# Eight experts in one order of load: which of them are split, and which one comes first

## The chip, the core and the metric

The program runs on one core of one Trainium2 chip. The metric is device time in microseconds (us) of one execution, from the first to the last instruction with what lies around it. Four compute engines work side by side, each in its own fixed order: TensorE (PE, with its weight loads as PEld), VectorE (DVE), ScalarE (ACT) and GpSimd (POOL). SyncE (SP) issues nearly all transfers, also in a fixed order. An instruction that has to wait holds up everything behind it on its own engine.

## The reference

256 tokens of width 1024 pass two blocks of two layers. The change touches the last stage alone, a layer with eight experts, of which each token takes the two with the largest logits:

```python
def swiglu(x, w_gu, w_down):
    g, u = jnp.split(x @ w_gu, 2, axis=-1)
    return (jax.nn.silu(g) * u) @ w_down

def moe_ffn(x, router, w_gu, w_down):
    ...
    logits = (xt @ router).astype(jnp.float32)
    top_v, top_i = lax.top_k(logits, TOP_K)
    w = jax.nn.softmax(top_v, axis=-1)
    ...
    for e in range(N_EXPERTS):
        y = y + combine[:, e:e + 1] * swiglu(xt, w_gu[e], w_down[e])
```

An expert is 3 x 1024 x 3584 weights in fp32, that is 42 blocks of 1 MiB; all eight are 336 MiB (352.3 MB). For the inputs of this case the reference sends 63, 135, 103, 26, 69, 94, 6 and 16 tokens to experts 0 to 7, or, by size, 135, 103, 94, 69, 63 (expert 0), 26, 16 and 6.

## The kernel before

Everything ahead of the expert layer (two hybrid layers, a pooling layer, a dense layer, an attention layer) is the same in both kernels and takes the first 1100 us. Then `moe_layer` (L1555 and on) does this.

**Routing.** `Route.choose` ranks the logits of 128 tokens at a time; `place` gives each token its slot in its expert's list; `route_order` (L1174 to L1221) sorts the experts by load, makes the table `R` of slots and weights in the sorted order, and casts the sorted expert numbers into `ri` (L1212). SP reads a number from `ri` into a register (`value_load` in `begin`, L1363) and uses it as the address of that expert's weights. A constant `first` adds 1000 to the count of expert 0, so that expert 0 always takes place 0 of the order, whatever its load. Its address is therefore known without routing (`E.static`), and its loads stand in SP's queue ahead of any read of `ri`.

**Two ways to compute an expert.** A place in the order has a fixed number of slots.
- A *split* place (slots 128, or 128 and another 64 for the place of 192): the slots' rows of x are gathered by a product with a selection matrix (`gather_x`); each 1 MiB of weights is cut by ACT into a high part `whi` (L148) and by DVE into a low part `wlo` (L149), and PE multiplies in three passes (`mm3`, L210 to L212). The further 64 slots take two passes (`prod`, L1324 and L1325).
- An *unsplit* place (64 or 32 slots): fp32 weights go to PE as they were loaded, with two (64) or four (32) products side by side in the columns of the array (`prod_full`, L1333), and `fold` adds the partial sums on ACT and DVE.

Before, the places are: 0 (expert 0) split 128; 1 split 192; 2, 3, 4 split 128; 5 unsplit 64; 6, 7 unsplit 32. With the loads above the split places hold 63, 135, 103, 94, 69 and the unsplit ones 26, 16, 6. If any load exceeds its place, a branch at the end (`over`, L1647) computes the rest; here it isn't taken.

**Buffers and order.** Loads go round seven buffers of 1 MiB (`raw`); besides, `K.spare` sends one load in eight (more at the start) into places that are otherwise unused (the table at L1574). Split parts have four buffers each. Two generators run through the experts in steps of 512 hidden columns, each of three parts (gate, up, down; 21 parts for an expert): one over places 0 to 4, one over 6, 7, 5. The second is advanced by a rate per part of the first (`rate`, L1635: 0.4 during place 0, 1.4 during place 1, 0.48 then), which mixes unsplit parts among the split ones. A scheduler then fixes the order of each engine.

Of the kernel before, what the change touches and what calls it, by code (L numbers as in the profile page):

```python
# [9 lines left out]
F32 = mybir.dt.float32  # L10
# [8 lines left out]
KT = D // 128  # L19
# [32 lines left out]
def _consts():  # L52
# [36 lines left out]
    for g in range(2):  # L89
        for q in range(64):  # L90
# [9 lines left out]
                ("first", np.tile([1000.0] + [0.0] * 7, (128, 1))),  # L100
                ("lim", np.array([[128.0, 192, 128, 256, 256, 64, 32, 256]])),
# [1070 lines left out]
def route_order(K, pool, S):  # L1172
# [21 lines left out]
    cnt = sc(8)  # L1194
    nc.vector.tensor_tensor(cnt, Q[:, 1, :], cst("first"), op=OP.add)
# [69 lines left out]
def gather_x(K, pool, x, R, p, tl, n, between=None):  # L1265

    half = tl.kind == "h"
    dbl = 2 if n == 0 else 1
    nc = K.nc
    m = tl.m  # L1270
    xg = buffer(K, pool, f"xg{n}", 0, *([[128, KT, m], F32] if tl.full else [[128, KT, m // 64, 128], F32R]), dbl)
    if between is None:
        if tl.P is None:
            select(K, pool, R, p, tl)
        steps = [(k, t) for k in range(KT) for t in range(2)]
    else:
        select(K, pool, R, p, tl, [0])
        K.hold_at[K.loads + 2] = [K.last]
        steps = [(k, t) for t in range(2) for k in range(KT)]
    ps = {}  # L1280
    hold = []
    for k, t in steps:
        if between is not None and (k, t) == (4, 0):
            hold = [between()]
            select(K, pool, R, p, tl, [1])
        if t == 0 and k % 4 == 0:
            ps[k] = bank(K, "mm")[:, :4 * m].rearrange("p (a b) -> p a b", a=4)
        k0 = k - k % 4
        with behind(K, hold):
            nc.tensor.matmul(ps[k0][:, k % 4, :], x[:, t, k * 128:(k + 1) * 128], tl.P[:, t, :m],  # L1290
                             start=t == 0 and (between is None or k % 4 == 0),
                             stop=t == 1 and (between is None or k % 4 == 3))
        if t == 0 or k % 4 < 3:
            continue
        if tl.full:
            nc.scalar.activation(xg[:, k0:k0 + 4, :], ps[k0], AF.Copy)
        elif half:
            evac_hl(K, xg[:, k0:k0 + 4, 0, 0:64], xg[:, k0:k0 + 4, 0, 64:128], ps[k0])
        else:
            evac_hl(K, xg[:, k0:k0 + 4, 0, :], xg[:, k0:k0 + 4, 1, :], ps[k0])  # L1300
    tl.xg = xg
# [45 lines left out]
class Expert:  # L1347
    def __init__(self, p, tiles):
        self.p, self.tiles = p, [Tile(*t) for t in tiles]
        self.static = 0 if p == 0 else None  # L1350
        self.full = self.tiles[0].full


def run_experts(K, pool, A, x, R, ri, cw, y, experts, hook=None, last=False):
# [5 lines left out]
    def begin(E):  # L1360
        if E.static is None:
            with behind(K, K.line):
                e = nc.sync.value_load(ri[0:1, E.p:E.p + 1], min_val=0, max_val=NE - 1)  # L1363
        else:
# [194 lines left out]
def moe_layer(K, x, A, out, ps1, S):  # L1559
    nc = K.nc  # L1560
    with ExitStack() as es:
# [6 lines left out]
        with K.tc.tile_pool(name="exp", reuse_waits="tile", bufs=1) as ep:  # L1568
# [16 lines left out]
            gather_w(K, ep, cw, 0, E[0].tiles[0], 0)  # L1585
# [8 lines left out]
            E[1].tiles[1].sb = True  # L1594
            ahead = [(1, 0), (1, 1)]
            slots = {6: 0, 7: 32, 5: 64}

            def few():

                b = ep.tile([128, 2048], F32, name="box2", tag="box2")  # L1600
                xg = b[:, 0:1024].rearrange("p (k m) -> p k m", m=128)
                K.boxes["sgl"] = [b[:, c:c + 512] for c in (1024, 1536)]
                P = b[:, 1536:1792].rearrange("p (t m) -> p t m", t=2)
                for p, c in slots.items():
                    tl = E[p].tiles[0]
                    select(K, ep, R, p, tl)
                    for t in range(2):
                        nc.vector.tensor_copy(P[:, t, c:c + tl.m], tl.P[:, t, :tl.m])
                    gather_w(K, ep, cw, p, tl, f"l{p}")
                    tl.xg = xg[:, :, c:c + tl.m]  # L1610
                for k0 in range(0, KT, 4):
                    ps = bank(K, "mm").rearrange("p (a b) -> p a b", a=4)
                    for k in range(k0, k0 + 4):
                        for t in range(2):
                            nc.tensor.matmul(ps[:, k % 4, :], x[:, t, k * 128:(k + 1) * 128], P[:, t, :],
                                             start=t == 0, stop=t == 1)
                    nc.scalar.activation(xg[:, k0:k0 + 4, :], ps, AF.Copy)

            def boxes():
                b = [ep.tile([128, 2048], t, name=f"box{n}", tag=f"box{n}") for n, t in enumerate((F32R, F32))]  # L1620
                K.boxes["xg1"] = [b[0][:, 0:1024].rearrange("p (k o m) -> p k o m", o=1, m=128)]
                K.boxes["hT1"] = [b[0][:, c:c + 512].rearrange("p (k o m) -> p k o m", o=1, m=128) for c in (1024, 1536)]
                K.boxes["sg1"], K.boxes["sacc"] = [b[1][:, c:c + 512] for c in (0, 512)], [b[1][:, 1024:2048]]

            def hook(i):
                if i == 3:
                    few()
                if i == 4:
                    boxes()
                if 3 <= i < len(ahead) + 3:  # L1630
                    p, n = ahead[i - 3]
                    select(K, ep, R, p, E[p].tiles[n])
                if 4 <= i < len(ahead) + 4:
                    p, n = ahead[i - 4]
                    gather(K, ep, x, R, cw, p, E[p].tiles[n], n)  # L1635

            light, done, due = go([E[6], E[7], E[5]]), 0, 0.0
            rate = (0.4, 1.4, 0.48, 0.48, 0.48)
            for e, f in go([E[q] for q in (0, 1, 2, 3, 4)], hook, True):
                if E[5].tiles[0].xg is not None:  # L1640
                    due += rate[e.p]
# [5 lines left out]
            with K.tc.If(over > 0):  # L1647
                K.line = []
                rest = ((0, F1), (1, H(192)), (2, F1), (3, H(128)), (5, H(64)), (6, H(32)), (7, H(32)))
# [126 lines left out]
```

## Time and profile before

| what | value |
|---|---|
| runs | 2082.11, 2083.7, 2084.06 us; median 2083.7 us |
| profiled execution | 2082.68 us; its span 2080.7 us, so 1.98 us lie around the span |
| PE busy | 1998.4 us (96% of the span) |
| DVE, ACT busy | 1349.0 us (65%), 1029.1 us (49%) |
| moved from HBM | 520.73 MB, mean 251 GB/s over the span |
| expert layer | PE from about 1115 us on, the last loads issued at 2034.9 us |

The page's row of PE's busy share counts matmuls whose ends are modelled, so a share near 100% in a stretch doesn't say that PE did all it can there; the starts of its instructions, and how far apart they are, say more. The page's two rows of the DMA (busy share and GB/s in 40 slices) show two halves: some 170 GB/s up to 1100 us, and 320 to 420 GB/s after, where the expert weights are loaded.

### The profile page before, as it was taken

Reading aid. Unit: us, or ns where it says so; the run is one execution under the profiler, and the core shown is the slowest. Engines: PE = TensorE matmul, PEld = TensorE weight load, DVE = VectorE, ACT = ScalarE, POOL = GpSimd, SP = SyncE. Lnnn points to the kernel's source line nnn. Section 1 sums busy time; section 2 is a strip of 40 time slices with the busy share of each in tenths; the row PEclk is TensorE's granted clock in tenths of the full one; section 3 lists DMA queues with packets and bytes.
Section 4 is the critical chain, followed back from the end, with each engine's and each line's share of the span. In section 5 each row is a group of like instructions: output and inputs, shape, how many; then the busy total and the mean of one; then the engine's idle time right before and its main releaser. Section 6 shows DMA issues by size and latency. Waiting matters only on the chain. (4 is left out here: it accounts for less than half of the span.)

```text
span 2080.7 us, 28322 instructions
## 1 busy us (share of the span) xinstructions
PE 1998.4 (96%) x11287; PEld 1586.8 (76%) x11287; DVE 1349.0 (65%) x1722; ACT 1029.1 (49%) x1222; POOL 34.8 (2%) x39
## 2 busy tenths in 40 slices
PE   8999999999999899999899999999999999999996
PEld 7879998888999899988778876567666766665664
DVE  6866545876545644566659775656577777656756
ACT  6654444664444433345335665445355555545543
POOL 0000000000001100000000000000000000000000
PEclk9999999999999999999878999999999999999998
DMA  9434554535555455550406799999899999999993
GB/s 342 156 102 150 176 182 177 182 108 187 175 200 182 163 182 183 170 193 21 167 1 243 323 374 385 370 349 401 337 401 371 392 423 380 355 346 364 373 379 104
DMA packets 137851, 523.69 MB, mean 252 GB/s; under 512 B 12016, under 2 KB 44144, under 8 KB 94832
## 3 DMA queue, kind: packets, MB, share of 16 engines
q1 hardware_dynamic: 137568, 521.75, 66.5%
q8 instruction: 90, 1.47, 0.3%
q14 instruction: 49, 0.40, 0.1%
q10 hardware_dynamic: 144, 0.07, 0.0%
HBM read 520.73 MB, written 1.05 MB: 251 GB/s over the span
## 5 line engine op out<-in xcount | busy, mean ns | idle before, releaser
L149 DVE TENSOR_TENSOR wlo<-raw,whi 128x2048 fp32r<-128x2048 f32 (+2 forms) x346 | 739.8, 2159 | 295.4 <-ACT whi L148 295.0
L148 ACT ACTIVATE whi<-raw 128x2048 fp32r<-128x2048 f32 (+2 forms) x348 | 619.3, 1808 | 265.5 <-issue 63.0
L211 PE MATMUL acc<-wlo,hT 128*128 128x512 f32 x624 | 245.9, 394 | 2.4 <-DVE wlo L149 2.4
L212 PE MATMUL acc<-whi,hT 128*128 128x512 f32 x624 | 243.6, 391 | 0.0
L211 PE MATMUL mm<-wlo,xg 128*128 128x512 f32 x560 | 226.9, 405 | 11.7 <-DVE wlo L149 11.7
L210 PE MATMUL mm<-xT,whi 128*128 128x256 f32 (+1 forms) x824 | 237.0, 288 | 0.8 <-ACT mqk L458 0.4
L210 PE MATMUL acc<-whi,hT 128*128 128x512 f32 x624 | 236.0, 393 | 1.3 <-ACT whi L148 1.3
L210 PE MATMUL mm<-whi,xg 128*128 128x512 f32 x560 | 226.9, 405 | 8.3 <-ACT whi L148 4.4
L212 PE MATMUL mm<-xT,wlo 128*128 128x256 f32 (+1 forms) x824 | 234.4, 285 | 0.0
L211 PE MATMUL mm<-xT,whi 128*128 128x256 f32 (+1 forms) x824 | 233.8, 284 | 0.3
L212 PE MATMUL mm<-whi,xg 128*128 128x512 f32 x560 | 222.4, 397 | 0.4 <-DVE xg L226 0.4
L210 PEld LDWEIGHTS mm<-xT,whi 128*128 128x128 f32 (+1 forms) x824 | 155.6, 189 | 4.8 <-issue 1.1
L211 PEld LDWEIGHTS mm<-xT,whi 128*128 128x128 f32 (+1 forms) x824 | 155.7, 189 | 3.3 <-DVE xT L677 1.1
L212 PEld LDWEIGHTS mm<-xT,wlo 128*128 128x128 f32 (+1 forms) x824 | 155.6, 189 | 1.3 <-issue 0.7
L210 PEld LDWEIGHTS mm<-whi,xg 128*128 128x128 f32 x560 | 106.8, 191 | 56.2 <-issue 16.4
L211 PEld LDWEIGHTS acc<-wlo,hT 128*128 128x128 f32 x624 | 117.2, 188 | 38.4 <-issue 10.0
L211 PEld LDWEIGHTS mm<-wlo,xg 128*128 128x128 f32 x560 | 107.1, 191 | 48.2 <-DVE wlo L149 17.0
L210 PEld LDWEIGHTS acc<-whi,hT 128*128 128x128 f32 x624 | 116.7, 188 | 31.3 <-issue 5.0
L212 PEld LDWEIGHTS acc<-whi,hT 128*128 128x128 f32 x624 | 117.2, 188 | 28.8 <-issue 5.0
L212 PEld LDWEIGHTS mm<-whi,xg 128*128 128x128 f32 x560 | 107.4, 192 | 27.4 <-issue 5.0
L211 PE MATMUL mx<-xT,whi 128*128 128x256 f32 x416 | 117.7, 283 | 0.0
L212 PE MATMUL mx<-xT,wlo 128*128 128x256 f32 x416 | 117.7, 283 | 0.0
(387 smaller groups left out, 2998.1 us busy)
## 6 DMA issues: line engine op xcount, KB each, us to landing
raw<-in_moe_gu_dram SPq DMA_DIRECT2D x193, 1024.0 KB, 7.7
raw<-in_moe_dn_dram SPq DMA_DIRECT2D x95, 1024.0 KB, 7.6
raw<-in_w_up_dram SPq DMA_DIRECT2D x32, 1024.0 KB, 5.7
raw<-in_w_down_dram SPq DMA_DIRECT2D x32, 1024.0 KB, 5.0
spare<-in_moe_gu_dram SPq DMA_DIRECT2D x31, 1024.0 KB, 7.4
raw<-in_w_in_dram SPq DMA_DIRECT2D x26, 1024.0 KB, 5.5
raw<-in_ffn_w_gu_dram SPq DMA_DIRECT2D x22, 1024.0 KB, 4.9
spare<-in_moe_dn_dram SPq DMA_DIRECT2D x15, 1024.0 KB, 7.5
```

The source lines that it names most:

```text
L148: nc.scalar.activation(h, d, AF.Copy)
L149: K.lo.tensor_tensor(l, d, h.bitcast(F32), op=OP.subtract)
L210: nc.tensor.matmul(ps, l[0], r[0], start=start, stop=False)
L211: nc.tensor.matmul(ps, l[0], r[1], start=False, stop=False)
L212: nc.tensor.matmul(ps, l[1], r[0], start=False, stop=stop)
```

## The change

Expert 0 loses its own place: `first` goes, all eight experts are sorted by load, and the places become split 192, 128, 128, 128 and unsplit 64, 64, 32, 32. With the loads of this case they hold 135, 103, 94, 69 and 63, 26, 16, 6. Expert 0 with its 63 tokens moves from a split place of 128 to an unsplit one of 64. The `spare` places go, and so does the early, interleaved gather of expert 0; the first expert, too, has its number read from `ri`. The selection for the unsplit experts is made in two goes (`few` for 6, 7 and for 4, 5), and the rate is 1.5 during place 0 and 0.86 then.

```diff
-                ("first", np.tile([1000.0] + [0.0] * 7, (128, 1))),
-                ("lim", np.array([[128.0, 192, 128, 256, 256, 64, 32, 256]])),
+                                ("lim", np.array([[192.0, 128, 128, 128, 64, 64, 32, 32]])),
...
-    cnt = sc(8)
-    nc.vector.tensor_tensor(cnt, Q[:, 1, :], cst("first"), op=OP.add)
+    cnt = Q[:, 1, :]
...
-        if E.static is None:
-            with behind(K, K.line):
-                e = nc.sync.value_load(ri[0:1, E.p:E.p + 1], min_val=0, max_val=NE - 1)
-        else:
-            e = E.static
+        with behind(K, K.line):
+            e = nc.sync.value_load(ri[0:1, E.p:E.p + 1], min_val=0, max_val=NE - 1)
...
-            spare = [("xg0", 2), ("more", 1), ("box0", 1), ("box1", 1), ("box2", 1)]
-            for q in range(56):
-                for n in range(q > 0, (5, 3)[q] if q < 2 else 2):
-                    K.spare[K.loads + (8 if q == 0 else 12 + 8 * q) + n] = lambda n=n: ep.tile(
-                        [128, 2048], F32, name=f"spare{n}", tag=spare[n][0], bufs=spare[n][1])
             K.iota = S.cst("iota")
-            E = [Expert(p, t) for p, t in enumerate(([F0], [F0, H(128)], [F0], [F0], [F0], [(0, "s")], [(0, "q")], [(0, "q")]))]
-            gather_x(K, ep, x, S.Q, 0, E[0].tiles[0], 0, lambda: S.place(1))
-            K.hold_at[K.loads + 3] = [K.last]
+            E = [Expert(p, t) for p, t in enumerate(([F0, H(128)], [F0], [F0], [F0], [(0, "s")], [(0, "s")], [(0, "q")],
+                                                     [(0, "q")]))]
+            S.place(1)
             R, ri, cw = route_order(K, pool, S)
...
             def hook(i):
-                if i == 3:
-                    few()
...
+                if i == 0:
+                    few(few_xg[1], 6, 7)
+                if i == 2:
+                    few(few_xg[0], 4, 5)
+
+            light, done, due = go([E[6], E[7], E[4], E[5]]), 0, 0.0
+            for e, f in go(E[:4], hook, True):
+                if E[6].tiles[0].xg is not None:
+                    due += 0.86 if e.p else 1.5
```

In the rows of the order below, a line of the changed kernel is one lower than the same line before up to L1190, two lower from there to the gather and some twenty-odd lower in the experts (L1333 before is L1311 after).

On SP, the first expert's loads stood behind the two small loads of the routing, ahead of any read of `ri`; the `spare` rows are loads too. Before:

```order
L1116 DMA route<-in_c_dram 128x408
L1117 DMA route<-in_router_dram 128x64
L133 DMA raw<-in_moe_gu_dram 128x2048 x8
L133 DMA spare_9877<-in_moe_gu_dram 128x2048
L133 DMA spare_9883<-in_moe_gu_dram 128x2048
L133 DMA spare_9916<-in_moe_gu_dram 128x2048
L133 DMA spare_9922<-in_moe_gu_dram 128x2048
L133 DMA spare_9962<-in_moe_dn_dram 128x2048
L133 DMA raw<-in_moe_dn_dram 128x2048
L133 DMA raw<-in_moe_gu_dram 128x2048 x2
L1646 TENSOR_LOAD ri
```

After, in the same place of SP's queue:

```order
L1115 DMA route<-in_c_dram 128x400
L1116 DMA route<-in_router_dram 128x64
L1339 TENSOR_LOAD ri
L1339 ISA x2
L132 ISA
L132 DMA raw<-in_moe_gu_dram 128x2048
```

The read of `ri` (TENSOR_LOAD) now stands ahead of every load of expert weights.

On DVE, between the count of the slots (L1168, a copy into `route`) and the cast of the sorted numbers into `ri` (L1212). Before, the split of a block of expert 0's weights (L149) and the gathered rows (L226) stand inside this chain:

```order
L1256 CAST Pr<-P 128x256
L149 TENSOR_TENSOR wlo<-raw,whi 128x2048
L1189 TENSOR_TENSOR route<-route 128x2
L1191 TENSOR_TENSOR route<-route 128x16
L1199 TENSOR_TENSOR route<-route 128x64
L1200 TENSOR_TENSOR route<-route 128x64
L1192 TENSOR_TENSOR route<-route 128x16
L1201 TENSOR_TENSOR route<-route 128x64
L1193 TENSOR_TENSOR route<-route 128x16
L1202 TENSOR_TENSOR route<-route 128x64
L1204 TENSOR_REDUCE route<-route 128x8
L226 TENSOR_TENSOR xg_9620<-mm,xg_9620 128x4x128
```

After, the same chain from the count of the slots on (L1167 is that copy):

```order
L1167 COPY route<-acc 128x8
L1554 COPY iota<-route 128x128
L1184 TENSOR_TENSOR route<-route 128x2
L1197 TENSOR_TENSOR route<-route 128x64
L1198 TENSOR_TENSOR route<-route 128x64
L1186 TENSOR_SCALAR route<-route 128x2
L1199 TENSOR_TENSOR route<-route 128x64
L1187 RECIPROCAL route<-route 128x2
L1200 TENSOR_TENSOR route<-route 128x64
L1188 TENSOR_TENSOR route<-route 128x2
L1190 TENSOR_TENSOR route<-route 128x16
L1202 TENSOR_REDUCE route<-route 128x8
```

No split and no gathered rows stand in it any more; they come behind `ri`.

On ACT, at the end of the layer: `ye` are the finished rows of an expert, scaled for the last product; `whi` of 1024 and 512 columns are the last blocks of the last split expert. Before:

```order
L148 ACTIVATE whi<-spare_15998 128x2048
L1490 ACTIVATE ye<-acc,cs 128x512
L225 ACTIVATE hT_16004<-mm 128x4x128
L148 ACTIVATE whi<-raw 128x1024 x2
L148 ACTIVATE whi<-raw 128x512 x4
L1490 ACTIVATE ye<-acc,cs 128x512 x2
L1646 TENSOR_LOAD ri
```

After:

```order
L1316 ACTIVATE fu<-mm 64x512
L147 ACTIVATE whi<-raw 128x2048
L147 ACTIVATE whi<-raw 128x1024 x2
L147 ACTIVATE whi<-raw 128x512 x4
L1464 ACTIVATE ye<-acc,cs 128x512 x4
L1603 TENSOR_LOAD ri
```

The rows `ye` of the last unsplit expert stood ahead of the last splits; they now stand behind them, with those of the last split expert.

## Rows read from the trace of the kernel before

**Rows 1.** Busy time by stretch: us, PE, PEld, DVE, ACT, POOL, clock, DMA share, GB/s

```profile
1116.00:1307.00 191.00, 191.00 (x978) 144.20 (x979) 143.14 (x154) 118.03 (x103) 0.00 (x0) 1.00 0.86 344
...
1567.00:1738.00 171.00, 167.72 (x802) 112.44 (x800) 123.98 (x94) 99.67 (x81) 0.00 (x0) 1.00 0.98 395
1738.00:1920.00 182.00, 173.12 (x749) 115.74 (x751) 118.33 (x84) 93.63 (x73) 0.00 (x0) 0.97 0.94 359
```

**Rows 2.** PE's waits from 1116 to 2058 us: total, times, longest

```profile
PE mm L211 <- DVE wlo L149: 11.7, 9, 1.8
PE mm L210 <- ACT whi L148: 4.4, 5, 1.7
```

**Rows 3.** SP's longest wait from 1000 us on: total, times, longest

```profile
SPq L133 <- DVE wlo L149: 373.0, 141, 14.4
```

**Rows 4.** PE's timeline, split and unsplit: start, us, line, out<-in, weights, shape, count

```profile
1645.22 1.06 PE L1333 MATMUL acc<-spare,hTl 128*32 128x512 f32 x8
...
1646.79 0.39 PE L212 MATMUL mm<-whi,xg 128*128 128x512 f32 x1
...
1651.57 0.39 PE L212 MATMUL mm<-whi,xg 128*128 128x512 f32 x1
1651.89 1.94 PE L1333 MATMUL mm<-raw,box 128*64 128x512 f32 x8
1653.76 0.66 PE L1430 MATMUL mm<-ident,sg 128*128 128x128 f32 x4
```

**Rows 5.** PE's timeline: the gather of a place, sixteen products

```profile
1161.75 2.03 PE L1615 MATMUL mm<-box,x 128*128 128x128 f32 x16
```

**Rows 6.** SP's timeline: the first loads of the expert layer

```profile
1004.74 24.85 SPq L133 DMA_DIRECT2D raw<-in_moe_gu_dram  x8
1101.15 1.93 SPq L133 DMA_DIRECT2D spare<-in_moe_gu_dram  x4
```

**Rows 7.** All engines' timeline, 1110.5 to 1119 us: routing, and PE's first split product

```profile
1111.06 0.17 DVE L1168 COPY route<-acc 128x8 f32<-128x8 f32 x1
...
1111.81 2.29 DVE L149 TENSOR_TENSOR wlo<-raw,whi 128x2048 fp32r<-128x2048 f32 x1
...
1114.91 0.44 PE L210 MATMUL mm<-whi,xg 128*128 128x512 f32 x1
...
1115.21 0.68 DVE L226 TENSOR_TENSOR xg<-mm,xg 128x512 fp32r<-128x512 f32 x1
...
1117.70 0.16 DVE L1212 CAST ri<-R 1x16 int32<-1x16 f32 x1
...
1118.54 1.92 ACT L148 ACTIVATE whi<-raw 128x2048 fp32r<-128x2048 f32 x1 [3.01 <-PE mm L212]
```

**Rows 8.** The read of ri (L1646): ns min/median/max, start

```profile
L1646 SPq TENSOR_LOAD <-ri x1: 484/484/484, 1118.6 to 1118.6; - x1
```

**Rows 9.** Loads into raw, 1200 to 2060 us, from issue to landing

```profile
DMA to landing us min/median/max: 4.3/7.6/13.2
```

**Rows 10.** PE's timeline behind a wait, 2030 to 2034 us; idle time in brackets

```profile
2030.62 0.50 PE L211 MATMUL mm<-wlo,xg 128*128 128x512 f32 x1 [1.82 <-DVE wlo L149]
...
2031.45 0.63 PE L211 MATMUL mm<-wlo,xg 128*128 128x512 f32 x1
...
2034.01 0.63 PE L211 MATMUL mm<-wlo,xg 128*128 128x512 f32 x1
```

**Rows 11.** Busy time by stretch, as rows 1

```profile
1180.00:2034.00 854.00, 827.73 (x3976) 554.78 (x3975) 568.80 (x463) 455.18 (x392) 0.00 (x0) 0.99 0.95 375
1640.00:1720.00 80.00, 80.00 (x367) 52.51 (x368) 53.81 (x36) 42.00 (x32) 0.00 (x0) 1.00 1.00 412
```

**Rows 12.** DMA from 1101 to 2035 us: all packets; the issues of gate and up into spare places

```profile
DMA packets 47396, 343.38 MB, mean 368 GB/s; under 512 B 5232, under 2 KB 5232, under 8 KB 5612
...
spare<-in_moe_gu_dram SPq DMA_DIRECT2D x31, 1024.0 KB, 7.4
```

**Rows 13.** SP's timeline: the last loads of weights

```profile
2030.59 4.32 SPq L133 DMA_DIRECT2D raw<-in_moe_dn_dram  x6
```

More of the change, by code (lines that the diff above doesn't have):

```diff
@@ L1262, in gather, with gather_x @@
     gather_w(K, pool, cw, p, tl, n)
-def gather_x(K, pool, x, R, p, tl, n, between=None):
-    half = tl.kind == "h"
+def gather_x(K, pool, x, R, p, tl, n):
     dbl = 2 if n == 0 else 1
@@ L1270, in gather_x @@
     m = tl.m
[L1271 to L1275, printed above, removed]
-    else:
[L1277 to L1298, printed above, removed]
+    xg = buffer(K, pool, f"xg{n}", 0, [128, KT, m // 64, 128], F32R, dbl)
+    select(K, pool, R, p, tl)
+    for k0 in range(0, KT, 4):
+        ps = bank(K, "mm")[:, :4 * m].rearrange("p (a b) -> p a b", a=4)
+        for k in range(k0, k0 + 4):
+            for t in range(2):
+                nc.tensor.matmul(ps[:, k % 4, :], x[:, t, k * 128:(k + 1) * 128], tl.P[:, t, :m],
+                                 start=t == 0, stop=t == 1)
+        if tl.kind == "h":
+            evac_hl(K, xg[:, k0:k0 + 4, 0, 0:64], xg[:, k0:k0 + 4, 0, 64:128], ps)
         else:
-            evac_hl(K, xg[:, k0:k0 + 4, 0, :], xg[:, k0:k0 + 4, 1, :], ps[k0])
+            evac_hl(K, xg[:, k0:k0 + 4, 0, :], xg[:, k0:k0 + 4, 1, :], ps)
     tl.xg = xg
@@ L1349, in __init__ @@
         self.p, self.tiles = p, [Tile(*t) for t in tiles]
-        self.static = 0 if p == 0 else None
         self.full = self.tiles[0].full
@@ L1593, in moe_layer @@
             go = lambda *a: run_experts(K, ep, A, x, R, ri, cw, y, *a)
[L1594 to L1604, printed above, removed]
+            E[0].tiles[1].sb = True
@@ new lines, in moe_layer @@
+            b = [ep.tile([128, 2048], t, name=f"box{n}") for n, t in enumerate((F32R, F32, F32))]
+            K.boxes["xg1"] = [b[0][:, 0:1024].rearrange("p (k o m) -> p k o m", o=1, m=128)]
+            K.boxes["hT1"] = [b[0][:, c:c + 512].rearrange("p (k o m) -> p k o m", o=1, m=128) for c in (1024, 1536)]
+            K.boxes["sg1"], K.boxes["sacc"] = [b[1][:, c:c + 512] for c in (0, 512)], [b[1][:, 1024:2048]]
+            K.boxes["sgl"] = [b[2][:, c:c + 512] for c in (1024, 1536)]
+            few_xg = b[2][:, 0:1024].rearrange("p (k m) -> p k m", m=128), ep.tile([128, KT, 64], F32, name="xgq")
@@ L1605, in few @@
+            def few(xg, *ps):
+                w = xg.shape[2]
+                P = ep.tile([128, 2, 128], F32, name="PL")[:, :, :w]
+                for c, p in enumerate(ps):
                     tl = E[p].tiles[0]
+                    o = slice(c * tl.m, (c + 1) * tl.m)
                     select(K, ep, R, p, tl)
                     for t in range(2):
-                        nc.vector.tensor_copy(P[:, t, c:c + tl.m], tl.P[:, t, :tl.m])
+                        nc.vector.tensor_copy(P[:, t, o], tl.P[:, t, :tl.m])
@@ L1616, in few @@
                                              start=t == 0, stop=t == 1)
[L1617 to L1623, printed above, removed]
@@ L1625, in hook @@
-            def hook(i):
-                if i == 3:
-                    few()
[L1628 to L1638, printed above, removed]
@@ L1639, in moe_layer @@
-            for e, f in go([E[q] for q in (0, 1, 2, 3, 4)], hook, True):
-                if E[5].tiles[0].xg is not None:
-                    due += rate[e.p]
+                    nc.scalar.activation(xg[:, k0:k0 + 4, :], g, AF.Copy)
+            def hook(i):
+                if i == 0:
[6 more added lines that the diff above has]
+                    due += 0.86 if e.p else 1.5
@@ L1648, in moe_layer @@
                 K.line = []
-                rest = ((0, F1), (1, H(192)), (2, F1), (3, H(128)), (5, H(64)), (6, H(32)), (7, H(32)))
+                rest = ((0, H(192)), (1, F1), (2, F1), (4, H(64)), (5, H(64)), (6, H(32)), (7, H(32)))
                 for _ in go([Expert(p, [t]) for p, t in rest]):
```

8 lines of the change are left out of this document (3 added, 5 removed).

## The prediction

> **What bounds the kernel now.** I read the busy time by stretch first, because the whole change lies behind 1100 us. From 1116 to 1307 us PE shows no idle time while the DMA runs at 344 GB/s; from 1738 to 1920 us PE is busy 173 of 182 us at 359 GB/s [rows 1]. The DMA is seldom the end of the chain: over 80 us it delivers 412 GB/s with PE still full, and the mean of the whole layer is 368 to 375 GB/s [rows 11, 12]. PE's waits come next, and they name a split part that isn't ready (11.7 us on `wlo`, 4.4 us on `whi`), no load [rows 2]. SP, last, spends 373 us waiting until a split frees a buffer [rows 3]: loads wait for PE, through DVE and the buffers. So PE sets the pace of the layer, the loads follow with some 10% in hand (412 against 368), and what is taken from PE is worth its time only until the loads are used up.
>
> **The change, part by part.** All sums are made on the profiled execution: its span is 2080.7 us, its time 2082.68, so 2.0 us are added at the end. The median of the runs is 1.0 us above its time.
>
> *Expert 0 moves from split to unsplit.* Removed: 336 products of gate and up (14 blocks x 8 x 3) and 168 of down (7 x 8 x 3), together 504 of 128x512. From 1646.79 to 1651.57 us PE starts 21 of them, 0.2276 us apart [rows 4], so 504 x 0.2276 = 114.7 us. Added: 42 blocks of 1 MiB at 64 slots. One takes from the split product at 1651.57 to the transposes at 1653.76 us, less that product's own 0.23 us: 1.96 us [rows 4], and 42 x 1.96 = 82.3 us. Difference -32 us, all of it on PE, which sets the end. With it go 42 splits of 1.9 us on ACT and 2.3 us on DVE; those engines have idle time, so the direct worth is nothing, but a fifth of the 210 split blocks can no longer be late: a fifth of the 16 us that PE waits for them [rows 2] is 3 us, and a slowed clock behind each such wait (below) makes it -4 us (0 to -10).
>
> *Expert 0's loads wait for the routing.* Before, eight blocks were loaded at 1005 to 1030 us and the next ones issued at 1101.15 us [rows 6], and PE started on them at 1114.91 us [rows 7]. After, `ri` comes first. From the count at 1111.06 to the cast at 1117.70 us are 6.6 us; one split (2.2 us of DVE's time) and two gathered rows (0.6 us each) leave the chain [rows 7], so `ri` is there at 1114.3 us. Reading it takes 0.5 us [rows 8], the check and the first issue about as long: first load at 1115.4 us. Landing takes 4.3 to 7.6 us [rows 9]; DMA is idle then, so I take the low end, 1119.7 us. Then one block is split, 1.9 us on ACT and 2.3 us on DVE [rows 7]: PE runs from 1123.9 us on, +9 us (up to +12 with the median landing). PE is idle or on small gathers for some 9 us ahead of it. Behind a stop of under 2 us at 2030.62 us its products start 0.427 us apart, from 2031.45 to 2034.01 us [rows 10], twice the usual pitch, hence at 1.2 instead of 2.4 GHz. I add +2 us (0 to 3) for such a stretch here. What fills the gap is a gain: the first expert's gathers now stand in it. Before, those of the second expert ran inside the stream, 1.8 us for sixteen products [rows 5] and some 0.4 us with them, for two tiles: -4 us. Sum of the start: +7 us.
>
> *No spare places.* The loads into spare places (31 of gate and up [rows 12], and those of down beside them) go, and the ring has seven buffers instead of eight. A load takes 7.6 us [rows 9], at 2.8 us for 1 MiB (1.0486 MB at 375 GB/s [rows 11]) 2.7 are on their way at a time; of seven buffers 4.3 are left for blocks that wait or are being split, instead of 5.3. SP's 373 us of waiting [rows 3] says that the ring is mostly full. I take +2 us (0 to 10).
>
> *A new mix.* During place 0 a part is 40 products (9.1 us) and 1.5 unsplit parts at 32 slots. Such a part is two blocks of 1.0 us [rows 4] and 0.1 us each to begin, so the whole is 12.4 us, 12.8 with 0.4 us of transposes, for 5 MiB (5.24 MB): 409 GB/s. Then some 12 parts of place 1 run beside the rest of the 32-slot experts: 24 products (5.5 us) and 0.86 x 2.2 us, 7.4 us, with transposes 7.7 us for 3.72 MiB (3.9 MB): 506 GB/s. The DMA gives 412 [rows 11], so a part takes 9.5 us: 1.8 us more, 21 us for 12 parts. Against that stand blocks loaded ahead: seven buffers and four split ones, up to 11 MiB or 23 us of PE's work. I take +7 us (0 to 21), nearer to the low end because the ring is mostly full before [rows 3]. Then 64-slot parts: 5.5 + 0.86 x 3.9 + 0.3 = 9.2 us for 3.9 MB, 424 GB/s if PE never waits: just above what the rows show, so nothing of the burst is made good later.
>
> *The end.* The finished rows of the last unsplit expert stand behind the last splits on ACT. Its last half block on PE is 0.9 us [rows 4], then the scaling and four additions; most of it lies beside the last split expert's. +3 us (0 to 6).
>
> Edits with one answer: the limits and `first` remove one small DVE operation; the selection in two goes has the same count of instructions. Nothing to add.
>
> Sum: -32 - 4 + 7 + 2 + 7 + 3 = **-17 us**: span 2063.7, time **2066** us.
>
> **A rule against it.** The 80 us at 412 GB/s [rows 11] show what this core can draw alone. The Trainium skill, "DMA: Bandwidth & Descriptors", section "Where 436 GB/s comes from", says that for transfers from HBM a core's share of the memory, about 358 GB/s, is the limit, not the 435 GB/s of the fabric. By that figure 352.3 MB would take an estimated 984 us. The trace disagrees with the rule for a core that runs by itself. As a mechanism of this kernel, a stream no faster than the 359 GB/s of 1738 to 1920 us [rows 1] takes 981 us; with the first issue at 1115.4 and the 45.8 us that now lie between the last issue (2030.59 + 4.32 = 2034.9 us [rows 13]) and the span's end, it gives a time of 2144 us. PE, not the DMA, was the limit in that stretch, so I give it 0.02.
>
> **The rivals.**
> 1. *The loads become the bound, slower.* Now 343.4 MB go in 934 us; after, 352.3 MB must go from 1115.4 us on, since nothing is loaded ahead of the routing. The span is 1115.4 + 352.3 MB / rate + 45.8 us. It equals 2080.7 at 352.3 / 919.5 = 383 GB/s; below that the kernel is slower. With seven buffers, with unsplit blocks that hold theirs until PE has used them, and the 375 GB/s of the long stretch [rows 11], it is 939.5 us: span 2100.7, time **2103**. For: no higher rate than 375 is shown over more than 171 us. Against: it was reached with PE as the limit, and 395 GB/s stand over 171 us [rows 1]. Chance 0.18.
> 2. *Swallowed.* The burst costs its full 21 us and the ring 6: -32 - 4 + 7 + 6 + 21 + 3 = +1 us, the gain is used up, the loads run at 383 GB/s. Time **2084**. For: the burst and the 64-slot parts both ask for more than 412. Against: 390 GB/s would do for the forecast. Chance 0.12.
> 3. *More comes back.* The ring is full when the burst comes, the end is hidden, PE's waits halve: +9 - 32 - 4 - 10 = -37 us, time **2046**. For: each of these low ends follows from a row. Against: 352.3 MB in the 882 us that are left for them need 399 GB/s from first to last. Chance 0.18.
> 4. *It doesn't do what it says.* Place 4 has 64 slots and gets 63 tokens. Two more, by rounding in the layers ahead, and the branch at the end computes all the rests: seven experts of 42 MiB, 308 MB, at 412 GB/s over 700 us more. Chance 0.02.
>
> **How the numbers follow.** Forecast 0.48 (its own range 2052 to 2084), rivals 0.18, 0.12, 0.18, 0.02, and 0.02 for the slow stream. With every term at its low end the sum is -37, as in rival 3, time 2046; with every term at its high end -32 + 0 + 11 + 10 + 21 + 6 = +16, time 2099. I take 2044 to 2103; outside lie half of rival 1, the two rare ones and a little of rival 3. A measurement of this kernel tells 0.2% (4 us) from no change, so faster is below 2079.5, slower above 2087.9. Faster: 0.46 of the forecast, 0.18 of rival 3 and 0.02 of rival 2, 0.66. Same: 0.02 and 0.08, 0.10. Slower: 0.18, 0.02, 0.02 and 0.02, 0.24.
>
> **What would show it.** PE's first split product near 1122 us, and its even run from 1124 us on. The first load of weights at about 1115.4 us. 168 split blocks of 2048 columns (or their parts) on DVE, not 210. The DMA at 385 to 410 GB/s over the layer, near 412 while the 32-slot experts end. Waits of PE on split parts below 16 us; waits on loads (an unsplit product or ACT's `whi` behind a transfer) would be new and would be rival 1. The forecast is wrong if PE's stream starts later than 1127 us, if the rate of the loads stays below 383 GB/s, or if the stretch from PE's start to its last product isn't some 25 us shorter than the 942 us of before.

## The result, and the profile after

| | before | after |
|---|---|---|
| median of the runs | 2082.9 us (2081.3 to 2084.1) | 2026.4 us (2025.0 to 2028.8) |
| span of the profiled execution | 2080.7 us | 2023.0 us |
| first split product of the expert layer on PE | 1114.91 us | 1109.37 us |
| last product of the kernel starts at | 2063.33 us | 2006.57 us |

The ratio is 0.973, with an interval of 0.9715 to 0.9746: 56 us less, where the forecast was 17 us less (2066 us) and the range ended at 2044 us. The direction was right, the size was not: the time lies below the range. The medians below leave out one run of the mix 1.6, 0.4, 1.0 (experiment 6), which took 4795.9 us for a reason that isn't known.

The span is 57.7 us shorter. PE's first split product comes 5.5 us earlier (the forecast had it 9 us later), the stream from there to the last product is some 51 us shorter (forecast: 26), and what follows the last product is about 1 us shorter. From the first split product to the last product, first before, then after (us, PE, PEld, DVE, ACT, POOL, clock, DMA share, GB/s, the columns of [rows 1]):

```profile
1114.91:2063.33 948.42, 920.99 (x4414) 627.25 (x4413) 644.69 (x562) 511.38 (x440) 0.00 (x0) 0.99 0.91 358
```

```profile
1109.37:2006.57 897.20, 877.70 (x4207) 550.21 (x4208) 555.35 (x497) 439.45 (x401) 0.00 (x0) 0.99 0.95 389
```

PE's busy time falls by 43.3 us and its idle time from 27.4 to 19.5 us. The 942 us that the prediction names for the stream of before is the length of its window from 1116 to 2058 us; from product to product it is 948.4 us.

The stretches of the expert layer after, with the same columns:

```profile
1360.00:1530.00 170.00, 159.68 (x814) 100.45 (x812) 115.96 (x104) 89.92 (x82) 0.00 (x0) 0.99 0.99 408
1530.00:2000.00 470.00, 464.29 (x2048) 276.70 (x2044) 286.92 (x217) 228.34 (x185) 0.00 (x0) 1.00 0.98 399
1125.00:2000.00 875.00, 857.29 (x4120) 534.84 (x4119) 540.73 (x475) 430.67 (x390) 0.00 (x0) 0.99 0.96 391
```

PE still sets the pace (857 of 875 us). The DMA gives 391 GB/s over the layer and 408 over 170 us. The only stretch in which PE stands still to any extent is 1360 to 1530 us, 10.3 us, where the 32-slot experts end beside place 1. From 1530 us on it is idle for 5.7 of 470 us. The same stretch of before:

```profile
1530.00:2055.00 525.00, 503.71 (x2261) 336.20 (x2260) 353.80 (x255) 282.66 (x223) 0.00 (x0) 0.98 0.93 366
```

There it is idle for 21.3 of 525 us. PE's waits after, from 1125 us on (total, times, longest), answering to [rows 2]:

```profile
PE acc L210 <- DVE wlo L148: 5.2, 7, 1.6
PE mm L210 <- DVE wlo L148: 4.2, 5, 1.8
PE acc L209 <- ACT whi L147: 2.7, 2, 2.1
PE mm L209 <- ACT whi L147: 1.7, 1, 1.7
```

They sum to 13.8 us. Two of them make up PE's longest stop, in two parts with one product between them, at 1459.74 and 1462.07 us. The timelines of ACT and PE there, after:

```profile
1457.30 0.59 ACT L1316 ACTIVATE box<-mm 64x512 f32<-64x512 f32 x1 [10.63 <-PE mm L1311]
1457.79 1.90 ACT L147 ACTIVATE whi<-raw 128x2048 fp32r<-128x2048 f32 x1
```

```profile
1459.74 0.50 PE L209 MATMUL mm<-whi,xg 128*128 128x512 f32 x1 [1.66 <-ACT whi L147]
...
1462.07 0.80 PE L210 MATMUL mm<-wlo,xg 128*128 128x512 f32 x1 [1.82 <-DVE wlo L148]
```

The split that PE lacks stands on ACT behind the sum of an unsplit product (`box`), for which ACT has waited 10.63 us until PE ran that product. No load ends either wait. Before, a stop of the same kind, here behind the SiLU of a split product (`sg`):

```profile
1847.91 0.60 ACT L1405 ACTIVATE sg<-mm 128x512 f32<-128x512 f32 x1 [6.80 <-PE mm L212]
1848.41 7.30 ACT L148 ACTIVATE whi<-raw 128x2048 fp32r<-128x2048 f32 x4
```

```profile
1852.69 0.50 PE L211 MATMUL mm<-wlo,xg 128*128 128x512 f32 x1 [1.82 <-DVE wlo L149]
```

ACT's waits for loads are new (from 1125 us on; before it has none from 1116 us on):

```profile
ACT whi L147 <- DMA raw<-in_moe_gu_dram: 67.6, 33, 5.9
ACT whi L147 <- DMA raw<-in_moe_dn_dram: 8.7, 9, 2.7
```

SP's waits after, from 1125 us on, answering to [rows 3]:

```profile
SPq L132 <- PE mm L1311: 252.7, 76, 13.4
SPq L132 <- DVE wlo L148: 218.9, 101, 6.7
```

SP now waits longest until PE has used an unsplit block, no longer until DVE has split one. The loads start like this (timelines of DVE, SP, ACT and PE, in this order; answering to [rows 6, 7]):

```profile
1091.00 0.17 DVE L1167 COPY route<-acc 128x8 f32<-128x8 f32 x1
...
1093.94 0.15 DVE L1210 CAST ri<-R 1x16 int32<-1x16 f32 x1
```

```profile
1095.19 30.82 SPq L132 DMA_DIRECT2D raw<-in_moe_gu_dram  x13
```

```profile
1100.06 1.91 ACT L147 ACTIVATE whi<-raw 128x2048 fp32r<-128x2048 f32 x1 [8.46 <-DMA raw<-in_moe_gu_dram]
```

```profile
1109.37 0.77 PE L209 MATMUL mm<-whi,xg 128*128 128x512 f32 x1
```

The count copy that [rows 7] show at 1111.06 us is at 1091.00 us: the routing is done 20 us earlier. Nearly all of that lies in the attention ahead of it, which the prediction never looked at.

**Where the attention gained them.** Both traces run alike up to about 1015 us. A later stretch, first of before, then of after:

```profile
1030.00:1062.00 32.00, 31.64 (x110) 23.74 (x110) 10.68 (x47) 11.71 (x44) 0.00 (x0) 0.52 0.09 33
```

```profile
1030.00:1062.00 32.00, 31.95 (x203) 25.15 (x203) 18.97 (x74) 15.98 (x57) 0.00 (x0) 1.00 0.00 1
```

PE is busy all the time in both, but before it starts 110 products, after 203: the granted clock is 0.52 and 1.00, nearly all of the stretch at 1.2 GHz before. The same six products of the attention, first before, then after:

```profile
1035.21 1.54 PE L869 MATMUL mx<-vv,npT 128*128 128x64 f32 x6
```

```profile
1034.79 0.78 PE L868 MATMUL mx<-vv,npT 128*128 128x64 f32 x6
```

What stands ahead of the slow stretch in the kernel before (timelines of ACT, DVE and PE):

```profile
1024.62 1.91 ACT L148 ACTIVATE whi<-raw 128x2048 fp32r<-128x2048 f32 x1 [2.10 <-PE mm L212]
```

```profile
1026.95 2.28 DVE L149 TENSOR_TENSOR wlo<-raw,whi 128x2048 fp32r<-128x2048 f32 x1
1029.15 0.28 DVE L403 CUSTOM_DVE_ANT_0 nsm<-acc,c 128x128 f32<-128x128 f32 x1
```

```profile
1030.03 0.33 PE L862 MATMUL acc<-ident,nsm 128*128 128x128 f32 x1 [0.90 <-DVE small L403]
```

This is the split of expert 0's first block. With a known address its load went at 1005 us [rows 6], so its split could go early, and the scheduler put it ahead of a step of the attention's softmax (L403). DVE comes to that step at 1029.15 us; after, without the split, it comes at 1025.45 us. PE stops, and the clock falls. From the first product of L857 (L856 after) at 1026.24 us to the last transposes of L449 at 1085.60 us are 59.4 us; after, 1024.49 to 1068.59 us, 44.1 us. That is 15.3 of the 20 us; 1.8 us are gone by 1026 us, and the rest behind 1085 us, in a wait of PE for `yT` and a short slow stretch.

### The profile page after: what moved, and what is told of

It reads as the page before. It is cut to its first block, busy times and chain, and to the rows that moved or that the text cites. A ratio compares the mean times of both kernels' runs of the same rounds, so it can differ in the third digit from the quotient of the medians.

```text
span 2023.0 us, 27962 instructions
## 1 busy us (share of the span) xinstructions
PE 1943.7 (96%) x11119; PEld 1502.8 (74%) x11119; DVE 1262.7 (62%) x1693; ACT 958.3 (47%) x1187; POOL 35.0 (2%) x39
## 5 line engine op out<-in xcount | busy, mean ns | idle before, releaser
L148 DVE TENSOR_TENSOR wlo<-raw,whi 128x2048 fp32r<-128x2048 f32 (+2 forms) x335 | 716.1, 2155 | 321.6 <-ACT whi L147 314.2
L147 ACT ACTIVATE whi<-raw 128x2048 fp32r<-128x2048 f32 (+2 forms) x337 | 600.3, 1805 | 311.9 <-DMA raw<-in_moe_gu_dram 76.1
L210 PE MATMUL acc<-wlo,hT 128*128 128x512 f32 x568 | 224.7, 396 | 5.2 <-DVE wlo L148 5.2
L211 PE MATMUL acc<-whi,hT 128*128 128x512 f32 x568 | 221.7, 391 | 0.0
L209 PE MATMUL acc<-whi,hT 128*128 128x512 f32 x568 | 215.7, 393 | 2.7 <-ACT whi L147 2.7
L209 PE MATMUL mm<-whi,xg 128*128 128x512 f32 x448 | 183.2, 409 | 4.4 <-ACT whi L147 1.7
L210 PE MATMUL mm<-wlo,xg 128*128 128x512 f32 x448 | 180.8, 404 | 4.2 <-DVE wlo L148 4.2
L211 PE MATMUL mm<-whi,xg 128*128 128x512 f32 x448 | 177.5, 396 | 0.0
L209 PEld LDWEIGHTS acc<-whi,hT 128*128 128x128 f32 x568 | 105.9, 188 | 31.7 <-issue 5.7
L211 PEld LDWEIGHTS acc<-whi,hT 128*128 128x128 f32 x568 | 106.7, 188 | 25.0 <-issue 3.3
L209 PEld LDWEIGHTS mm<-whi,xg 128*128 128x128 f32 x448 | 85.5, 191 | 47.1 <-issue 16.3
L210 PE MATMUL mx<-xT,whi 128*128 128x256 f32 x416 | 117.7, 283 | 0.0
L209 PE MATMUL mx<-xT,whi 128*128 128x256 f32 x416 | 117.7, 283 | 0.0
L210 PEld LDWEIGHTS mm<-wlo,xg 128*128 128x128 f32 x448 | 85.6, 191 | 38.0 <-issue 12.3
```

The source lines that it names most:

```text
L147: nc.scalar.activation(h, d, AF.Copy)
L148: K.lo.tensor_tensor(l, d, h.bitcast(F32), op=OP.subtract)
L209: nc.tensor.matmul(ps, l[0], r[0], start=start, stop=False)
L210: nc.tensor.matmul(ps, l[0], r[1], start=False, stop=False)
L211: nc.tensor.matmul(ps, l[1], r[0], start=False, stop=stop)
```

## The experiments

Times are medians of the runs; the kernel before is at 2082 to 2083 us beside each of them.

**1. The kernel before, without the two early splits in the attention.** The loads stay where they are.

```diff
-        K.hold_at[K.loads + 2] = [K.last]
+        K.hold_at[K.loads] = K.hold_at[K.loads + 1] = K.hold_at[K.loads + 2] = [K.last]
```

> The kernel before, with one edit: the splits of expert 0's first two blocks are held until the first selection of rows, as that of the third already was; its eight early loads stay at 1005 us. In the kernel before these two splits lie on ACT (1024.62 us, 1.91 us) and DVE (1026.95 and 1073.03 us, 2.3 us each) between the steps of the attention, whose products run at half clock from 1032 to 1062 us; without them PE's order in the attention is that of the changed kernel. Theory A (the splits in the queues of ACT and DVE, and the order that goes with them, cost the clock): the attention runs at full clock, the count copy comes at about 1091 instead of 1111.06 us, the first split product between 1095 and 1103 us (two more splits of 2.3 us on DVE ahead of it), time 2063 to 2071. Theory B (the 8 MiB of loads beside the attention cost the clock): nothing moves, 2081 to 2085.

Measured: **2067.0 us**, ratio 0.993 (0.991 to 0.995). Its stretch:

```profile
1030.00:1062.00 32.00, 31.95 (x202) 24.84 (x200) 18.85 (x73) 17.83 (x60) 0.00 (x0) 1.00 0.00 1
```

The clock stays at 2.4 GHz, the count copy comes at 1096.78 us (later than the 1091 us of theory A, as the two held splits now stand ahead of it on DVE), and the first split product at 1101.73 us. One line of the kernel before is worth 15 us; theory A holds.

**2 and 3. The changed kernel, with early loads nobody needs, and then with two early splits nobody needs as well.** The last two lines of the edit are in the second kernel only.

```diff
+            for q in range(7):
+                src = A["moe_gu"][0, q // 2, q % 2].rearrange("p (k n) -> p k n", k=4)
+                v = wload(K, src, 4, 512)
+                if q < 2:
+                    wsplit(K, v, 4, 512)
             S.place(1)
```

> The changed kernel, with seven blocks of weights loaded at the place where the kernel before loads expert 0's eight (about 1004 us), into the same seven buffers; nobody reads them. Nothing else differs on PE, ACT and DVE. Theory A (splits): the count copy stays at 1091 us and the time at 2026 (2023 to 2030). Theory B (traffic): the attention falls to half clock as in the kernel before, the count copy comes at about 1111 us, time 2041 to 2047.

> As the run with seven unused early loads, and two of the blocks are also split at once on ACT and DVE, as in the kernel before; nobody reads the parts. Theory A (splits): half clock in the attention's last part comes back, wholly or in part: count copy at 1098 to 1112 us, time 2034 to 2048. Theory B (traffic): as the run without the splits, within 5 us of it, at 2041 to 2047.

Measured: **2027.8 us** with the loads alone (the changed kernel: 2026.4), **2040.5 us** with the splits. The stretch of the first, then of the second:

```profile
1030.00:1062.00 32.00, 31.68 (x194) 24.07 (x192) 18.35 (x73) 16.64 (x63) 0.00 (x0) 1.00 0.00 1
```

```profile
1030.00:1062.00 32.00, 30.38 (x107) 23.34 (x108) 12.44 (x46) 13.28 (x47) 0.00 (x0) 0.52 0.00 1
```

7 MiB of loads beside the attention cost nothing in time that these runs tell, though the count copy comes at 1093.45 instead of 1091.00 us. Two splits cost 13 us, and the count copy moves on to 1109.08 us. In the second kernel PE's stop ahead of the slow stretch is 2.50 us:

```profile
1031.60 2.94 PE L861 MATMUL acc<-ident,nsm 128*128 128x128 f32 x9 [2.50 <-ACT nsm L403]
```

Theory A again. One thing stays open: with the splits the scheduler also puts the attention's products in another order (the output products that start at 1042.59 us after start at 1058.32 us before). No run has the one without the other, so the runs show what the splits and their order do together.

**4. The swap undone in the changed kernel.** Place 4, with its 63 tokens, is split at 128 slots again; places 5 to 7 stay unsplit, at 64, 32 and 32; the limits and the selection follow. The first run uses 0.4 unsplit parts for each split one behind place 0, the second the changed kernel's own 0.86.

```diff
-([F0, H(128)], [F0], [F0], [F0], [(0, "s")], [(0, "s")], [(0, "q")],
+([F0, H(128)], [F0], [F0], [F0], [F0], [(0, "s")], [(0, "q")],
...
-            light, done, due = go([E[6], E[7], E[4], E[5]]), 0, 0.0
-            for e, f in go(E[:4], hook, True):
+            light, done, due = go([E[6], E[7], E[5]]), 0, 0.0
+            for e, f in go(E[:5], hook, True):
                 if E[6].tiles[0].xg is not None:
-                    due += 0.86 if e.p else 1.5
+                    due += 0.4 if e.p else 1.5
```

> The changed kernel, with the expert in place 4 (63 tokens) split in a tile of 128 slots again, as expert 0 was, so that five experts are split and three unsplit; all else is that of the changed kernel (no early loads, no place for expert 0, seven buffers; 0.4 unsplit parts for each split one after place 0, so that the unsplit experts end at the same point). Theory A (the swap is worth what its own instructions cost): 504 split products at 0.2276 us against 42 unsplit blocks at 1.96 us, 32 us, and a few for late parts: 2057 to 2063. Theory C (the swap is worth more, since each split product also carries the small waits and slowed stretches of a stream of split parts): 2066 to 2078.

> As the run with place 4 split again, but with the changed kernel's own mix, 0.86 unsplit parts for each split one behind place 0: the three unsplit experts then end in place 2, and the rest, some 47 parts, is split parts alone. In the runs so far such a row of split parts alone shows no waits to speak of, while stretches with 0.4 to 0.7 show 5% and more. Theory A (the swap's own instructions are worth 37 to 44 us, and the 62 us of the first run with it held 20 us of its mix): 2063 to 2072. Theory C (the swap itself is worth 60 us): 2083 to 2092.

Measured: **2088.9 us** with 0.4, **2061.7 us** with 0.86. The first is beyond both theories, and the second shows what the first left out: the same expert products in another mix differ by 27 us. (3.9 of them lie ahead of the first split product, at 1111.48 and 1107.58 us; why it moved isn't known.) By the second, the swap is worth 35.3 us. That is inside theory A as the first run had it (2057 to 2063) and 1.3 us below the range that it was given for the second (2063 to 2072); theory C falls. The stretches behind 1530 us, first with 0.4, then with 0.86:

```profile
1530.00:2050.00 520.00, 496.45 (x2215) 336.51 (x2207) 358.29 (x243) 288.53 (x217) 0.00 (x0) 0.99 0.95 368
```

```profile
1530.00:1784.00 254.00, 248.05 (x1106) 149.93 (x1107) 155.95 (x118) 127.14 (x100) 0.00 (x0) 1.00 0.98 399
1784.00:2030.00 246.00, 246.00 (x1125) 203.10 (x1124) 214.59 (x129) 173.31 (x119) 0.00 (x0) 1.00 0.93 348
```

With 0.4, PE is idle for 23.6 us. With 0.86 the unsplit experts are done by 1784 us; from there split parts stand alone, DVE is busy 215 of 246 us, and PE shows no wait.

The runs so make a chain: 2082.7 us before; 2088.9 us with the places' new order, seven buffers and late loads, but five split experts in much the mix of before (0.4 behind the first place against 0.48); 2061.7 us by the mix; 2026.4 us by the swap. That is +6, -27 and -35 us.

**5. The ring.** The changed kernel with six buffers (`bufs=6`), and the kernel before without its spare places (the table that fills `K.spare` deleted).

> The changed kernel with a ring of six buffers for loaded blocks instead of seven. Theory A (the step of the prediction: a buffer less costs about 2 us, 0 to 10, since the ring is mostly full): 2026 to 2031. Theory B (a ring of seven is already what holds the loads back, since SP waits until PE has used an unsplit block for 253 us and until DVE has split one for 219 us): 2034 to 2050, with PE's waits on split parts above the 14 us of now.

> The kernel before without its spare places: all blocks go through the ring of seven, and nothing else changes. Theory A (as in the prediction, 8 buffers against 7 cost 2 us, 0 to 10): 2083 to 2090. Theory B (the ring holds the loads back): 2093 to 2110.

Measured: **2034.9 us** with six (8.5 us more than the changed kernel), **2088.2 us** without the spare places (6 us more than before, ratio 1.0026, 1.0014 to 1.0038). The first is in the range of theory B, although PE's waits on split parts don't rise above 14 us, as that theory asked; the second is in that of theory A. With six buffers ACT waits nearly twice as long for loads (140 against 76 us in the changed kernel):

```profile
ACT whi L147 <- DMA raw<-in_moe_gu_dram: 104.3, 47, 6.3
ACT whi L147 <- DMA raw<-in_moe_dn_dram: 36.2, 24, 5.4
```

The eighth place is worth 6 us, in the upper half of the prediction's 0 to 10; the seventh, more.

**6. The mix.** Other rates of unsplit parts in the changed kernel, the one line of `due` changed:

> The changed kernel with another mix: 1.6 unsplit parts for a split one in place 0 (1.5 before), 0.4 after it while 32-slot parts are left, 1.0 then (0.86 for both before). The prediction's term for the new mix was 7 us (0 to 21), for the stretch in which 32-slot parts run beside the 24-product parts of place 1; in the changed kernel PE waits some 10 us between 1409 and 1530 us. Theory A (these waits are that burst): they go, time 2017 to 2023. Theory B (they come from the order of ACT and DVE at the change of experts): they stay, 2024 to 2030.

> The changed kernel with 1.0 unsplit part for each split one all the way, so that place 0 takes 21 instead of 31 of the 32-slot parts and place 1 twice as many as now. Theory A (the burst costs): two times the burst, PE's waits on late parts 8 to 20 us longer, time 2034 to 2047. Theory B (the mix doesn't matter): 2024 to 2030.

> The changed kernel with 1.65 unsplit parts for a split one in place 0 and 0.82 behind it (1.5 and 0.86), so that 6 instead of 10 of the 32-slot parts are left for place 1. Theory A (the 10 us of PE's waits at 1409 to 1530 us are loads that come late for these): 2 to 4 us less, 2021 to 2025. Theory B (the mix of the changed kernel is the best there is: place 0 can't take more, as the run with 1.6 and 0.4 may have shown): 2026 to 2035.

> The changed kernel with 1.0 instead of 0.86 unsplit parts for each split one behind place 0 and 1.5 in place 0 as now: the unsplit experts end some ten split parts before the last. Theory A (one to one is the mix with the fewest late splits, and a row of split parts alone at the end has none): the waits from 1529 us on fall from 9 to 3 to 5 us, time 2019 to 2024. Theory B (the loads, which one to one asks for some 430 GB/s, take that back): 2025 to 2034.

| place 0 | behind it | time | PE idle from 1360 us on |
|---|---|---|---|
| 1.5 | 0.86 (the change) | 2026.4 us | 10.3 of 170, then 5.7 of 470 us |
| 1.65 | 0.82 | 2031.7 us | 11.7 of 240, then 1.8 of 405 us |
| 1.5 | 1.0 | 2037.1 us | 11.4 of 480 us from 1530 us on |
| 1.6 | 0.4, then 1.0 | 2035.8 us | 17.2 of 240, then 2.0 of 410 us |
| 1.0 | 1.0 | 2044.7 us | 19.5 of 240, then 5.7 of 410 us |

No other rate is better, and the times span 18 us. The first and the last of these runs, as their theories are listed above, lie above both of theirs; the second is in the range of theory A, the third in that of theory B. Less unsplit work in place 0 is dear (2044.7 us, or 8 us against 1.5 with the same 1.0 behind it), as the burst theory says; but the attempt to flatten the burst, 0.4 behind place 0, costs 9 us instead of gaining. Its stretch:

```profile
1360.00:1600.00 240.00, 222.76 (x1068) 152.55 (x1067) 162.56 (x128) 130.30 (x107) 0.00 (x0) 0.96 0.96 371
```

It asks for less from the DMA (371 GB/s against 409 in the changed kernel's same stretch) and waits more for splits (17 against 9 us). The loads alone don't set these waits. Of the 11 us that 1.0 behind place 0 costs, idle time explains 6, and products at half clock an estimated 4 more (17 against 8 us of them from 1125 to 2000 us, by the granted clock in steps of 5 us). Why it waits more is open.

**7. The kernel before, with the same unsplit parts laid otherwise.** `rate` is (0.4, 1.4, 0.72, 0.72, 0.0) instead of (0.4, 1.4, 0.48, 0.48, 0.48).

> The kernel before with its 64-slot parts laid otherwise: 0.72 for each split part in places 2 and 3 and none in place 4 (0.48 in all three before); the same work in all. Theory A (PE waits for a late split where two split parts stand back to back, because the next splits stand on ACT behind a step that waits for the first part's product; an unsplit part in between covers it): places 2 and 3 lose most of their waits, as the changed kernel with 0.86 has 9 us of them from 1529 us on against 25 us in the kernel before from 1534 us on; place 4, 21 split parts in a row, gains some 2.4 us of waits and 1.5 us of slowed products for many of them, 30 us or more: time 2090 to 2120. Theory B (waits go with the number of split blocks, as the prediction had it): waits and time stay, 2078 to 2087.

Measured: **2075.6 us**, ratio 0.9965 (0.9954 to 0.9977), faster by 7 us. Both theories fall. Waits don't go with the number of split blocks, which is the same; and split parts back to back, which theory A held to be the costly pattern, have none. Places 2 and 3, then place 4 alone:

```profile
1530.00:1926.00 396.00, 380.61 (x1716) 237.82 (x1715) 248.00 (x190) 196.49 (x163) 0.00 (x0) 0.98 0.97 387
1926.00:2045.00 119.00, 118.69 (x535) 97.07 (x534) 107.86 (x68) 84.20 (x59) 0.00 (x0) 1.00 0.85 322
```

PE is idle 15.4 of 396 us where parts are mixed at 0.72, and 0.3 of 119 us where split parts are alone.

**8. The start.** The changed kernel, with the first expert's second split held behind the gather:

```diff
-    nc.vector.tensor_reduce(tl.cs, pp[:, 256:258], axis=AX.X, op=OP.add)
+    w = nc.vector.tensor_reduce(tl.cs, pp[:, 256:258], axis=AX.X, op=OP.add)
+    if p == 0 and n == 0:
+        K.hold_at[K.loads + 1] = [w]
```

> The changed kernel with the split of the first expert's second block held until the first tile's gather is done; before, that split (2.3 us at 1105.20 us) stands on DVE ahead of the tile's second half, and PE waits for it twice, 1.57 us each. Theory A (the first split product waits for DVE's order): it comes 2 to 4 us earlier, near 1106 us, and the time is 2022 to 2025. Theory B (the second block is then late by as much): 2025 to 2029.

Measured: **2025.6 us**, no change (the changed kernel's runs are 2025.0 to 2028.8 us). The first split product comes at 1111.93 us, not earlier: PE now waits 2.4 us for the gathered rows elsewhere. Theory A isn't borne out; the time is in the range of theory B.

## Why the prediction was wrong, and what of it held

**Right: what bounds, and the swap.** PE sets the pace after as before, the loads follow at 391 GB/s, inside the 385 to 410 of the forecast, and rivals 1 and 2 didn't come; more came back than even rival 3 had (2046 us). The swap with its share of the late splits was priced at 36 us; undone with the same mix it is 35.3 us. DVE's split instructions behind 1095 us, after and then with the swap undone:

```profile
L148 DVE TENSOR_TENSOR wlo<-raw,whi 128x2048 fp32r<-128x2048 f32 (+1 forms) x172 | 382.2, 2236 | 116.6 <-ACT whi L147 109.3 <-PE mm L1303 7.0
```

```profile
L148 DVE TENSOR_TENSOR wlo<-raw,whi 128x2048 fp32r<-128x2048 f32 (+2 forms) x214 | 476.5, 2246 | 107.4 <-ACT whi L147 99.7 <-PE mm L1303 7.0
```

There are 172 and 214, 42 more, as counted. Counting instructions and taking each one's pitch from a stretch without waits is what worked: by the swap the stream from the first split product to the last product becomes 37.3 us shorter, 34.6 of PE's busy time (forecast 32) and 2.7 of its idle time (forecast 4). That the total agrees within 1 us is in part luck, as the stream also begins 1.8 us later. Of the other terms the forecast made a loss of 19 us, and they are a gain of 21 (2082.7 to 2061.7 us, the kernel with the swap undone). These 40 us are the miss. Some 16 of them lie ahead of the first split product (7.3 us earlier there, where the forecast had it 9 us later), and 24 in the stream (13.9 us shorter, where these terms made it 10 us longer). Two steps failed: one at the start, one in the mix.

The sign that the prediction gave to rival 1, ACT's `whi` behind a transfer, did appear (76 us of waits, none before), and the rival didn't: of ACT's waits little reaches PE, which waits 4.4 us for `whi` in all. It wasn't a sign of that rival.

**Wrong: "expert 0's loads wait for the routing", +7 us.** The chain from the count copy on was nearly right: 2.94 us to the cast of `ri` (forecast 3.2), 1.25 us to the first load (1.1), 4.9 us until ACT starts to split (4.3). The step that failed is its starting point. It took the count copy at 1111.06 us as given. But moving expert 0's loads behind the routing moves what follows them too, and two of their splits had stood in the attention, in the queues of ACT and DVE. The prediction counted the 42 splits that go, and wrote that "those engines have idle time, so the direct worth is nothing"; that holds for the mean and not for a split whose place was in front of a softmax that PE waits for. A stop of 0.9 us there is followed by 30 us at half the clock (with another order of the products, which no run parts from the split). The row of the clock from 1000 to 1110 us stood in the trace before; I read stretches only from 1116 us on. Runs 1 to 3 put 13 to 15 us on this, and the count copy comes 20 us earlier.

Some of that is lost again: between the first load and the first split product lie 14.2 us, not 8.5. The first split is done at 1104.3 us, 9.1 us behind the load's issue, but the gather, which I had booked as work that fills a gap, isn't: its second half leaves DVE at 1108.4 us, behind the splits (holding the second split back gained nothing, run 8). The 2 us of slowed products are there (ten of them, 0.43 us apart, from 1109.37 us on).

**Wrong: the mix, +7 us (0 to 21), and how the late splits were scaled.** This step took the mix as a demand on the DMA alone, which could only cost, and never priced what another mix does to PE's waits for splits. PE does stand still for 10.3 us between 1360 and 1530 us at 408 GB/s, where the burst was forecast, but that the size fits is luck: the longest stop, 3.5 us in two parts, hangs on ACT's order and on no load, as the lines above show, and asking less of the DMA there made the waits longer (experiment 6). Of the others only one, of 0.86 us at 1419.27 us, comes directly behind splits for which ACT waited for loads. The larger effect is in the long stretch behind: there PE's idle time falls from 21.3 to 5.7 us, and with the swap undone it is as low (5.95 us from 1530 to 2030 us), so it goes with the mix and not with the swap. With the swap undone, 0.4 against 0.86 moves the time by 27 us, more than the whole range of the term, and here it is a gain. I scaled the late splits by the number of blocks, a fifth; run 7 shows that the number isn't what counts.

What does count is not settled. Stretches of split parts alone have next to no waits. In the long stretch, with about 0.8 to 1.0 unsplit parts for each split one, 0.5 to 2.5% of the time is idle; with 0.4 to 0.72 it is 4 to 5%. From 1360 to 1600 us, just behind place 0, it is 5 to 8% with any rate of experiment 6. In most of the stops above 0.7 us that the traces show from 1530 us on, in the kernel before and in the run with 0.4, the split that PE lacks stands on ACT behind a step that has waited up to some 10 us for a product of PE; none of them comes behind a wait of ACT for a load. So the order on ACT is a likely cause; no run changes it by itself. Nor are the 24 us that the two mixes differ by in the stream all idle time: that makes 16 of them, and the rest isn't explained.

**The ring, +2 us:** 6 us by run 5, with the right sign and inside its bounds. **The end, +3 us:** not there. The last product starts 16.4 us before the span's end, against 17.4 before, and PE waits about 1 us for the finished rows of the last unsplit expert.

The rate rule that was weighed against the change fell on this trace too, with a core that runs by itself: 394 GB/s over the loads' 895 us, and 408 over 170 us, where the Trainium skill, "DMA: Bandwidth & Descriptors", section "Where 436 GB/s comes from", has some 358 GB/s as the limit of a core's share.

## What to carry to other kernels

When loads or splits are moved, look at what stood in the engines' queues where they were, not only at where they go: work of an "idle" engine can stand in front of the one step that PE waits for, and a stop of a microsecond can be followed by tens of microseconds at half the clock. Read the granted clock of every stretch ahead of the change before taking its time as given. A price by instruction counts and pitches came within some 3 us here, while the mix of two streams was worth nearly as much as the change itself (27 against 35 us); it has to be measured with the change undone under the same mix.

## What was new of the hardware

- A stop of PE of 0.9 us at 1030 us, and then some 30 us of small products at a granted clock of 0.52 with PE never idle. With the stop at 0.2 us and another order of products, the clock is 1.00 in the same stretch.
- Seven 1 MiB loads beside the attention, at 414 GB/s from 1008 to 1025 us, with no effect on the time that these runs tell (2027.8 against 2026.4 us) and a granted clock of 1.00 from 1030 to 1062 us as without them.
- 246 us of split parts in a row at 348 GB/s with DVE busy for 87% and PE without a wait in the profile.
